# An SSD mixer's decay masks: one add and ten biased exps per block instead of ten subtractions and one exp, a fused state recurrence, and both directions' inputs formed in a row

## The chip, the cores and the metric

The kernel runs as one program on one core of a Trainium2 chip. Times are device microseconds (us) of one execution; the metric is their median. TensorE (PE) does the matrix products, VectorE (DVE), ScalarE (ACT) and GpSimd (POOL) the rest, SyncE (SP) issues most transfers. Each engine takes its instructions strictly in the order in which the program gives them to it.

## The reference

One step of a two-layer hybrid model on 640 tokens (128 context tokens, 512 latent ones), in 32-bit floats. Layer 0 runs a bidirectional Mamba-2 SSD mixer and an attention mixer, layer 1 an RG-LRU; each is followed by a gated FFN. The change lies in the SSD mixer alone. It has 16 heads of width 64 in 2 groups, states of 64, and works in 5 chunks of 128 tokens:

```
acs = jnp.cumsum(dtc * a, axis=2)
seg = acs[:, :, :, None] - acs[:, :, None, :]
lmat = jnp.exp(jnp.where(tril, seg, -jnp.inf))
xdt = xc * dtc[..., None]
cb = jnp.einsum('bcqgn,bckgn->bcqkg', cc, bc)
y_diag = jnp.einsum('bcqkg,bcqkgh,bckghp->bcqghp', cb, lmat, xdt)
decay_end = jnp.exp(acs[:, :, -1:] - acs)
states = jnp.einsum('bckgn,bckgh,bckghp->bcghpn', bc, decay_end, xdt)
h = chunk_decay * h + states          # chunk after chunk, from h0
y_off = jnp.einsum('bcqgn,bcghpn,bcqgh->bcqghp', cc, prev, jnp.exp(acs))
```

The backward direction does the same on the flipped sequence, and the two y are added.

## The kernel before

Every 32-bit product is made of three matmuls on split operands (`mm3`, lines 470 to 472, 128x322 each). The input projection of the SSD mixer makes 8 blocks of x and 8 of the gate z, each of 128 features, in the order of a hand-written plan; one call of `mm3` is one tick of a clock that exists only while the program is written. Beside it run three generators, each of which gives up its turn with `yield n` for n ticks (the table `SSD` holds the n). So the order of work on each engine is fixed by ticks and by conditions such as "y_done", not by time: whatever a generator issues at a tick stands in the engines' queues there, whether its data are ready or not.

- `mask_terms` forms for each block t of two heads (i counts the blocks) and each direction d the decay mask E (128 x 1280: 2 heads, 5 chunks of 128x128). The cumulative sums come broadcast by a DMA on SP (E<-ad, 640 KB), DVE takes the column's value off each 128x128 piece and clips at 88 (L1016, 10 instructions per direction), ACT takes one exp of the whole (L1017), and DVE multiplies by CBm (L1022), the product of C and B with the triangle already in it (made at L982, one per chunk and group). POOL then adds the two directions into M (L69). For each even block, Cs (exp on ACT at L1036, product with C on POOL, L69) serves two blocks; its two buffers are free for the next pair when the y of the block before have read them.
- `states` forms for each pair of blocks and each direction xw (DVE, L1057) in a single buffer, 8 products into the PSUM bank "o" (L1064), turns the final states on PE (L1071, L1072), copies them out on ACT (`fin` L1068, `ends` L1075), and runs the recurrence over chunks on DVE: a product (L1079) and an add from PSUM (L1082) per chunk, 128x128 each.
- `y_terms` multiplies M and Cs with x and the states (PE L1107, L1113) into a wide PSUM tile, and DVE folds the result into X (L317), then times zt (L1123).

Around them on the same queues: for each x block, ACT starts the convolution (L520) and DVE adds three taps (L317), later ACT takes silu (L1152), PE transposes (L1138), ACT copies to xtk (L1140); for each z block ACT evacuates with silu (zt, L1160), which frees one of two PSUM banks `gh`; ACT splits each weight block (whi, L112), POOL makes the rest (wlo, L117). Pieces of the modulation vector are also made here: four column-blocks of products on PE (L332) into a small PSUM bank `mt`, added on DVE (L340), and at an end transposed (L347) and added to a bias (L352). `mt` tiles sit in two banks, "m" and "o"; one is free for the next user when the last reader is done.

Of the kernel before, what the change touches and what calls it, by code (L numbers as in the profile page):

```python
# [9 lines left out]
F32 = mybir.dt.float32  # L10
F32R = mybir.dt.float32r
AF = mybir.ActivationFunctionType
# [9 lines left out]
NT = S0 + NS  # L22
# [218 lines left out]
def tile_hybrid_step(ctx: ExitStack, tc: tile.TileContext, a, o):  # L241
# [618 lines left out]

    def softplus(pool, out, x, sign, n):

        t = pool.tile([128, 4, n], F32, name="sp", tag="xw", bufs=1)
        ax, e, z, p = [t[:, i] for i in range(4)]
        nc.scalar.activation(ax, x, AF.Abs)
        nc.scalar.activation(e, ax, AF.Exp, scale=-1.0)
        nc.vector.tensor_scalar(ax, e, 2.0, None, op0=OP.add)
        nc.vector.reciprocal(z, ax)
        nc.vector.tensor_mul(z, z, e)
        nc.vector.tensor_mul(ax, z, z)  # L870
        nc.vector.tensor_scalar(p, ax, 1.0 / 15, None, op0=OP.mult)
        for c in (13, 11, 9, 7, 5, 3):
            fma(p, p, 1.0 / c, ax, op0=OP.add, op1=OP.mult)
        fma(p, p, 1.0, z, op0=OP.add, op1=OP.mult)
        nc.vector.tensor_scalar(e, x, float(sign), 0.0, op0=OP.mult, op1=OP.max)
        fma(out, p, 2.0, e, op0=OP.mult, op1=OP.add)
# [26 lines left out]
    def ssd(ctx2, ps):  # L903
# [6 lines left out]
        CT = conv(pool, ps[1], "ssd_cw", "ssd_cb", 4, 9, 10, "CT", 1)  # L910
        nc.scalar.activation(BT, BT, AF.Silu)
        nc.scalar.activation(CT, CT, AF.Silu)
        dtT = pool.tile([32, NT], F32, name="dtT", tag="xw")

        def dt_out(p, c0, c1):
            nc.scalar.copy(dtT[:, c0:c1], p[:32])
# [4 lines left out]
        wst = pool.tile([128, 160], F32, name="wst")  # L921
        cd = pool.tile([128, 5, 2, 8], F32, name="cd")
        Btok = pool.tile([128, 5, 128], F32, name="Btok")
        CBm = pool.tile([128, 5, 2, 2, 128], F32, name="CBm")
        acsT = pool.tile([32, 640], F32, name="acsT", tag="xw")
        ad = dpool.tile([32, 640], F32, name="ad")
        xtk, zt, Ms, Cs = {}, {}, {}, {}
        k.y_done = 0
# [1 line left out]
        def col(v, c, d, t, h):  # L930
            i = 32 * c + 16 * d + 2 * t + h
            return v[:, i:i + 1]

        def prep():
            m = mtile()
            for c, (c0, c1) in enumerate(CHUNKS):
                nc.tensor.transpose(m[:, 32 * c:32 * c + 32], dtT[:, c0:c1], ident[:32, :32])
            x = k.ldt = pool.tile([128, 160], F32, name="dA")
            nc.vector.tensor_add(x.rearrange("p (c h) -> p c h", c=5), m[:, :160].rearrange("p (c h) -> p c h", c=5),
                                 dtb[:, None, :].to_broadcast([128, 5, 32]))  # L940
            softplus(pool, dt, x, 1, 160)
            nc.vector.tensor_mul(x.rearrange("p (c h) -> p c h", c=5), dt.rearrange("p (c h) -> p c h", c=5),
                                 nega[:, None, :].to_broadcast([128, 5, 32]))
            yield SSD[0]
            m, m2 = mtile(), mtile()
            for c in range(5):
                for d in range(2):
                    q = slice(32 * c + 16 * d, 32 * c + 16 * d + 16)
                    nc.tensor.matmul(m[:, q], tri[:, d], x[:, q], start=True, stop=True)
            nc.tensor.matmul(m2[:, :160], ones, x, start=True, stop=True)  # L950
            nc.scalar.copy(acs, m[:, :160])
            nc.vector.tensor_sub(wst, m2[:, :160], acs)
            mv = m2[:, :160].rearrange("p (c d g h) -> p c d g h", c=5, d=2, g=2)
            for g in range(2):
                nc.scalar.activation(cd[64 * g:64 * g + 64], mv[64 * g:64 * g + 64, :, :, g], AF.Exp)
            nc.scalar.activation(wst, wst, AF.Exp)
            nc.vector.tensor_mul(wst, wst, dt)
            nc.vector.tensor_scalar(x, dt, 1e-38, None, op0=OP.max)
            nc.scalar.activation(x, x, AF.Ln)
            nc.vector.tensor_sub(x, acs, x)  # L960
            yield SSD[1]
            m, m2 = mtile(), mtile()
            for c in range(5):
                t = m[:32, 128 * c:128 * c + 128] if c < 4 else m2[:32, :128]
                nc.tensor.transpose(t, acs[:, 32 * c:32 * c + 32], ident)
            nc.vector.tensor_copy(acsT[:, :512], m[:32])
            nc.vector.tensor_copy(acsT[:, 512:], m2[:32, :128])
            nc.scalar.dma_start(ad, acsT)
            yield SSD[2]
            m, m2 = mtile(), mtile()  # L970
            for c, (c0, c1) in enumerate(CHUNKS):
                t = m[:, 128 * c:128 * c + 128] if c < 4 else m2[:, :128]
                nc.tensor.transpose(t, BT[:, c0:c1], ident)
            nc.vector.tensor_copy(Btok[:, :4], m.rearrange("p (c n) -> p c n", c=4))
            nc.vector.tensor_copy(Btok[:, 4], m2[:, :128])
            yield SSD[3]
            for c, (c0, c1) in enumerate(CHUNKS):
                for g in range(2):
                    m = mtile()
                    r = slice(64 * g, 64 * g + 64)  # L980
                    nc.tensor.matmul(m[:, :128], BT[r, c0:c1], CT[r, c0:c1], start=True, stop=True)
                    nc.vector.tensor_mul(CBm[:, c, :, g], tri, m[:, None, :128].to_broadcast([128, 2, 128]))  # L982
                yield SSD[4]

        def heads(t, d, n, part, c0, nt):
# [4 lines left out]
        def mask_terms():  # L990
# [14 lines left out]
            for i, t in enumerate(order):  # L1005
                until2 = i - 1
                while k.y_done < until2:
                    yield 1
                es = pend.pop(t)
                if i + 1 < 8:  # L1010
                    load(order[i + 1])
                for d in range(2):
                    for h in range(2):
                        for c in range(5):
                            v = es[d][:, h, 128 * c:128 * c + 128]
                            nc.vector.tensor_scalar(v, v, col(k.ldt, c, d, t, h), 88.0, op0=OP.subtract, op1=OP.min)  # L1016
                    nc.scalar.activation(es[d], es[d], AF.Exp)  # L1017
                    yield SSD[5]
                for d in range(2):
                    for h in range(2):  # L1020
                        v = es[d][:, h].rearrange("p (c q) -> p c q", c=5)
                        nc.vector.tensor_mul(v, v, CBm[:, :, d, t // 4])  # L1022
                    yield SSD[6]
                if i % 2 == 0:
                    while k.y_done < i:
                        yield 1
                    cs = []
                    for d in range(2):
                        q = pool.tile([128, 2, 512], F32, name="Cs", tag="Cs", bufs=2)
                        for g in range(2):  # L1030
                            heads(t + 4 * g, d, 64, q[64 * g:64 * g + 64], 128, 512)
                        cs.append(q)
                    Cs[t] = Cs[t + 4] = cs
                    yield SSD[7]
                    for q in cs:
                        nc.scalar.activation(q, q, AF.Exp)  # L1036
                        for h in range(2):
                            pieces(nc.gpsimd, "tensor_mul", q[:, h], q[:, h], CT[:, S0:])
                mm = Ms[t] = pool.tile([128, 2, 640], F32, name="M", tag="M", bufs=2)
                for h in range(2):  # L1040
                    pieces(nc.gpsimd, "tensor_add", mm[:, h], es[0][:, h], es[1][:, h])
                yield SSD[8]
# [3 lines left out]
        def states():  # L1046

            for i in range(4):
                ts = (i, 4 + i)
                while not k.prepared or any(t not in xtk for t in ts) or k.y_done < 2 * i - 2:  # L1050
                    yield 1
                S = [[None] * 5, [None] * 5]
                for d in range(2):
                    xw = pool.tile([128, 2, 5, 2, 64], F32, name="xw", tag="xw", bufs=1)
                    for j, t in enumerate(ts):
                        w = wst.rearrange("p (c e h) -> p c e h", c=5, e=2)[:, :, d, 2 * t:2 * t + 2, None]
                        nc.vector.tensor_mul(xw[:, j], xtk[t].rearrange("p c (h e) -> p c h e", h=2),  # L1057
                                             w.to_broadcast([128, 5, 2, 64]))
                    yield SSD[9]
                    m = mtile("o")  # L1060
                    cs = (0, 1, 2, 3) if d == 0 else (0, 4, 3, 2)
                    for n, c in enumerate(cs):
# [13 lines left out]
                    for n in range(1, 4):  # L1076
                        c, c2 = cs[n], (cs[n] + 1 if d == 0 else cs[n] - 1)
                        s = S[d][c2] = pool.tile([128, 128], F32, name="S", tag="S", bufs=16)
                        nc.vector.tensor_mul(s.rearrange("p (h e) -> p h e", h=2),  # L1079
                                             S[d][c].rearrange("p (h e) -> p h e", h=2),  # L1080
                                             cd[:, c, d, 2 * i:2 * i + 2, None].to_broadcast([128, 2, 64]))
                        nc.vector.tensor_add(s, s, m[:, 128 * n:128 * n + 128])  # L1082
                    yield SSD[11]
                Ss[i] = S

# [875 lines left out]
```

## Time and profile before

| | |
|---|---|
| time, median of 3 runs | 2131.27 us (2123.99 to 2131.78) |
| profiled execution | 2128.0 us, span 2126.2 us |
| PE busy | 1891.4 us, 89% of the span |
| DVE busy | 1467.3 us, 69% |
| POOL busy | 1208.1 us, 57% |
| ACT busy | 964.2 us, 45% |

The span is what the trace covers; the time has 1.8 us more around it. An engine's busy share is a mean over all stages; the lines that the diff touches run between about 115 and 320 us of the span. In the rows below, a line such as `E<-E,dA` names the tile written and the tiles read, `x10` the instructions grouped, and the bracket the idle time of the engine before the group with what ended it.

### The profile page before, as it was taken

How to read it: one execution, taken by the hardware profiler on the slowest of the kernel's cores; microseconds unless marked ns; L12 is line 12 of the kernel's file. 1: busy time of each engine (PE TensorE's matmuls, PEld its weight loads, DVE VectorE, ACT ScalarE, POOL GpSimd, SP SyncE). 2: the span in 40 equal slices, each digit the busy share in tenths (PEclk: the TensorE clock that was granted, in tenths of full speed). 3: DMA queues.
4: the chain of work that ended last, by engine and by line, in shares of the span. 5: the costliest groups of instructions: out<-in, count | busy, mean ns of one | idle time of the engine just before them, and what ended most of it. 6: DMA issues, size and time to landing. Idle time of an engine off the chain costs nothing.

```text
span 2126.2 us, 33767 instructions
## 1 busy us (share of the span) xinstructions
PE 1891.4 (89%) x12665; PEld 1735.7 (82%) x12665; DVE 1467.3 (69%) x2486; ACT 964.2 (45%) x1671; POOL 1208.1 (57%) x1542
## 2 busy tenths in 40 slices
PE   6878889999999988999999997977778799999997
PEld 4767768888888878799889997977678799999986
DVE  3477755656664357687777876788857778777874
ACT  3454444454553334343333444766724444343445
POOL 3335454333343535466666775688755577766772
PEclk9889999999999999999999998989789899999998
DMA  9545432121113431444542222111111122222221
GB/s 267 165 156 164 149 110 63 49 54 48 49 45 124 131 117 64 136 130 153 178 145 70 60 84 79 53 39 45 40 50 41 37 79 82 86 76 70 60 85 65
DMA packets 255578, 196.60 MB, mean 92 GB/s; under 512 B 13837, under 2 KB 233816, under 8 KB 255288
## 3 DMA queue, kind: packets, MB, share of 16 engines
q1 hardware_dynamic: 252664, 184.59, 28.9%
q0 software_dynamic: 2528, 7.13, 1.4%
q8 instruction: 100, 1.64, 0.3%
q10 hardware_dynamic: 224, 2.73, 0.3%
q14 instruction: 62, 0.51, 0.1%
HBM read 187.50 MB, written 6.92 MB: 91 GB/s over the span
## 4 chain that ended last, share of the span: by engine, by line
PE 36%; DVE 11%; POOL 9%; ACT 4%; issue 4%; DMA 4%; POOLq 0%; DVEq 0%; ACTq 0%; SPq 0%
PE wide L470 10%; PE wide L471 10%; PE wide L472 10%; POOL t L69 4%; POOL wlo L117 4%; DMA wraw<-in_ffn_w_up_dram 4%; DVE ft L317 2%; PE mt L332 1%; PE gh L470 1%; DVE X L317 1%; PE gh L471 1%; PE gh L472 1%; DVE wsum L141 1%; DVE wraw L140 1%; DVE wsum L139 1%
## 5 line engine op out<-in xcount | busy, mean ns | idle before, releaser
L117 POOL TENSOR_TENSOR wlo<-wraw,whi 128x256 fp32r<-128x256 f32 (+1 forms) x845 | 715.7, 875 | 544.7 <-ACT whi L112 476.8
L470 PE MATMUL wide<-hhi,whi 128*128 128x322 f32 (+4 forms) x1072 | 352.5, 329 | 49.5 <-DVE X L317 23.0
L471 PE MATMUL wide<-hlo,whi 128*128 128x322 f32 (+4 forms) x1072 | 345.8, 323 | 3.7 <-DVE hlo L511 3.4
L472 PE MATMUL wide<-hhi,wlo 128*128 128x322 f32 (+4 forms) x1072 | 343.1, 320 | 0.0
L112 ACT CAST whi<-wraw 128x1024 fp32r<-128x1024 f32 (+2 forms) x263 | 220.1, 839 | 150.4 <-PE wide L472 71.9
L470 PEld LDWEIGHTS wide<-hhi,whi 128*128 128x128 f32 x1072 | 213.2, 199 | 66.4 <-issue 21.6
L470 PE MATMUL gh<-hhi,whi 128*128 128x322 f32 (+3 forms) x704 | 236.7, 336 | 9.1 <-ACT zt L1160 8.6
L471 PE MATMUL gh<-hlo,whi 128*128 128x322 f32 (+3 forms) x704 | 221.2, 314 | 1.3 <-DVE hlo L511 1.0
L472 PE MATMUL gh<-hhi,wlo 128*128 128x322 f32 (+3 forms) x704 | 220.5, 313 | 0.0
L471 PEld LDWEIGHTS wide<-hlo,whi 128*128 128x128 f32 x1072 | 212.6, 198 | 6.1 <-DVE hlo L511 5.3
L472 PEld LDWEIGHTS wide<-hhi,wlo 128*128 128x128 f32 x1072 | 212.4, 198 | 0.0
L470 PE MATMUL wide<-hidh,whi 128*128 128x322 f32 (+4 forms) x624 | 199.7, 320 | 2.2 <-DVE ft L1584 2.2
L471 PE MATMUL wide<-hidl,whi 128*128 128x322 f32 (+4 forms) x624 | 195.5, 313 | 1.6 <-DVE hidl L511 1.6
L472 PE MATMUL wide<-hidh,wlo 128*128 128x322 f32 (+4 forms) x624 | 195.4, 313 | 0.0
L317 DVE SCALAR_TENSOR_TENSOR ft<-ft,PC 128x643 f32<-128x643 f32 x160 | 168.2, 1072 | 37.3 <-ACT ft L1526 35.3
L470 PEld LDWEIGHTS gh<-hhi,whi 128*128 128x128 f32 (+1 forms) x704 | 134.0, 190 | 34.7 <-issue 21.3
L1526 ACT ACTIVATE ft<-ft,PC 128x644 f32<-128x644 f32 x80 | 74.0, 927 | 144.4 <-DVE ft L1591 133.4
L317 DVE SCALAR_TENSOR_TENSOR X<-wide,modc,X 128x128 f32<-128x128 f32 (+3 forms) x264 | 123.5, 511 | 19.8 <-PE wide L472 19.8
L471 PEld LDWEIGHTS gh<-hlo,whi 128*128 128x128 f32 (+1 forms) x704 | 133.8, 190 | 2.4 <-DVE hlo L511 1.2
L472 PEld LDWEIGHTS gh<-hhi,wlo 128*128 128x128 f32 (+1 forms) x704 | 133.6, 190 | 0.6
L470 PEld LDWEIGHTS wide<-hidh,whi 128*128 128x128 f32 x624 | 118.7, 190 | 15.9 <-issue 7.0
L112 ACT CAST shi<-wsum 128x512 fp32r<-128x512 f32 x120 | 72.8, 617 | 124.3 <-DVE wsum L141 111.4
(386 smaller groups left out, 4676.4 us busy)
## 6 DMA issues: line engine op xcount, KB each, us to landing
wraw<-in_ffn_w_up_dram SPq DMA_DIRECT2D x88, 512.0 KB
mraw<-in_w_mod_dram SPq DMA_DIRECT2D x80, 512.0 KB
wraw<-in_ssd_attn_w_in_dram SPq DMA_DIRECT2D x42, 512.0 KB
wraw<-in_ffn_w_down_dram SPq DMA_DIRECT2D x96, 192.0 KB
E<-ad SPq DMA_DIRECT2D x16, 640.0 KB
mraw<-in_w_mod_dram SPq DMA_DIRECT2D x32, 256.0 KB
wraw<-in_ssd_attn_w_out_dram SPq DMA_DIRECT2D x16, 512.0 KB
wraw<-in_lru_w_in_dram SPq DMA_DIRECT2D x16, 512.0 KB
```

The source lines that it names most:

```text
L69: getattr(eng, op)(out[:, c], a[:, c], b[:, c])
L112: self.nc.scalar.copy(hi, src)
L117: low.tensor_sub(lo[:, q], src[:, q], hi[:, q].bitcast(F32))
L139: v.tensor_sub(s[:, 1], a[:, :4], b[:, :4])
L140: v.tensor_add(b[:, :4], b[:, :4], b[:, 4:])
L141: v.tensor_sub(s[:, 0], b[:, :4], a[:, :4])
L317: nc.vector.scalar_tensor_tensor(out, in0, scalar, in1, op0=op0, op1=op1, **kw)
L332: nc.tensor.matmul(m[32 * j:32 * j + 32, :256], scp[:, kt, :], raw[:, j * 256:(j + 1) * 256], start=half is None or kt == 0, stop=half is ...
L470: nc.tensor.matmul(ps[:whi.shape[-1], p0:p0 + c1 - c0], whi, xhi[:, c0:c1], start=start, stop=False)
L471: nc.tensor.matmul(ps[:whi.shape[-1], p0:p0 + c1 - c0], whi, xlo[:, c0:c1], start=False, stop=False)
L472: nc.tensor.matmul(ps[:whi.shape[-1], p0:p0 + c1 - c0], wlo, xhi[:, c0:c1], start=False, stop=stop)
L1526: after(at, lambda: nc.scalar.activation(out, u, AF.Identity, scale=par(cw, 2 * NF + t), bias=par(cb, t)))
```

## The change

Four things change. CB now holds the product of C and B without the triangle (ACT copies it from PSUM), and a tile `none` (0 inside the triangle, -1e30 outside, per direction) is added to E by DVE, one instruction per direction. The subtraction becomes the bias of the exp, so ACT runs ten exps of 128x128 per direction in place of one of 128x1280. The recurrence is one instruction per chunk and head (product and add in one, reading PSUM, 128x64). And xw has two buffers, both directions are formed one after the other, and the products of direction 1 follow 2 ticks behind the chain of direction 0. Lines after the edits move by up to 8.

```diff
@@ softplus, allocations
-        t = pool.tile([128, 4, n], F32, name="sp", tag="xw", bufs=1)
+        t = pool.tile([128, 4, n], F32, name="sp", tag="xw", bufs=2 if n > 16 else 1)
-        CBm = pool.tile([128, 5, 2, 2, 128], F32, name="CBm")
+        CB = pool.tile([128, 5, 2, 128], F32, name="CB")
+        none = pool.tile([128, 2, 128], F32, name="none")
@@ prep
+            nc.vector.tensor_scalar(none, tri, 1.0, 1e30, op0=OP.subtract, op1=OP.mult)
-            nc.vector.tensor_sub(x, acs, x)
+            nc.vector.tensor_sub(x, x, acs)
-                    nc.vector.tensor_mul(CBm[:, c, :, g], tri, m[:, None, :128].to_broadcast([128, 2, 128]))
+                    nc.scalar.copy(CB[:, c, g], m[:, :128])
@@ mask_terms
                 for d in range(2):
+                    v = es[d].rearrange("p h (c q) -> p (h c) q", c=5)
+                    nc.vector.tensor_add(v, v, none[:, d, None, :].to_broadcast([128, 10, 128]))
+                for d in range(2):
                     for h in range(2):
                         for c in range(5):
                             v = es[d][:, h, 128 * c:128 * c + 128]
-                            nc.vector.tensor_scalar(v, v, col(k.ldt, c, d, t, h), 88.0, op0=OP.subtract, op1=OP.min)
-                    nc.scalar.activation(es[d], es[d], AF.Exp)
+                            nc.scalar.activation(v, v, AF.Exp, bias=col(k.ldt, c, d, t, h))
                     yield SSD[5]
                 for d in range(2):
                     for h in range(2):
                         v = es[d][:, h].rearrange("p (c q) -> p c q", c=5)
-                        nc.vector.tensor_mul(v, v, CBm[:, :, d, t // 4])
+                        nc.vector.tensor_mul(v, v, CB[:, :, t // 4])
                     yield SSD[6]
@@ states
+                xws = []
                 for d in range(2):
-                    xw = pool.tile([128, 2, 5, 2, 64], F32, name="xw", tag="xw", bufs=1)
+                    xw = pool.tile([128, 2, 5, 2, 64], F32, name="xw", tag="xw", bufs=2)
...
-                    yield SSD[9]
+                    xws.append(xw)
+                    yield SSD[9] if d else 2
+                for d, xw in enumerate(xws):
                     m = mtile("o")
...
                     for n in range(1, 4):
                         c, c2 = cs[n], (cs[n] + 1 if d == 0 else cs[n] - 1)
                         s = S[d][c2] = pool.tile([128, 128], F32, name="S", tag="S", bufs=16)
-                        nc.vector.tensor_mul(s.rearrange("p (h e) -> p h e", h=2),
-                                             S[d][c].rearrange("p (h e) -> p h e", h=2),
-                                             cd[:, c, d, 2 * i:2 * i + 2, None].to_broadcast([128, 2, 64]))
-                        nc.vector.tensor_add(s, s, m[:, 128 * n:128 * n + 128])
+                        for h in range(2):
+                            e = slice(64 * h, 64 * h + 64)
+                            fma(s[:, e], S[d][c][:, e], cd[:, c, d, 2 * i + h:2 * i + h + 1],
+                                m[:, 128 * n + 64 * h:128 * n + 64 * h + 64])
                     yield SSD[11]
```

**First place.** ACT's queue where the first masks are made (the silu of an x block lies between the two directions), before:

```order
L735 ACTIVATE lv<-lv 128x2
L1017 ACTIVATE E<-E 128x1280
L1152 ACT_TABLE_LOAD
L1152 ACTIVATE X<-X 128x644
L1017 ACT_TABLE_LOAD
L1017 ACTIVATE E<-E 128x1280
L1068 COPY fin<-mt 128x128
L1140 COPY xtk<-wide 128x640
```

and after the change:

```order
L735 ACTIVATE lv<-lv 128x2
L1021 ACTIVATE E<-E,dA 128x128 x10
L1159 ACT_TABLE_LOAD
L1159 ACTIVATE X<-X 128x644
L1021 ACT_TABLE_LOAD
L1021 ACTIVATE E<-E,dA 128x128 x10
L1147 COPY xtk<-wide 128x640
L1075 COPY fin<-mt 128x128
```

The silu keeps its place behind the first direction's exps, which are now ten; on PE the state products (L1064, now L1071) have moved from two ticks ahead of the transposes of that X (L1138, now L1145) to behind them.

**Second place.** PE at the third y pass (tile M_1739, the first block of the second pair). Before, the transposes of an X block come first and the pass begins 5 ticks later:

```order
L1071 MATMUL mt_1801<-ident_68,ends1_463 128x128
L1072 MATMUL mt_1801<-ident_68,fin_1742 128x128
L470 MATMUL wide_1703<-hhi7_81,whi_1383 128x322
L471 MATMUL wide_1703<-hlo7_89,whi_1383 128x322
L472 MATMUL wide_1703<-hhi7_81,wlo_1384 128x322
L470 MATMUL wide_1703<-hhi7_81,whi_1383 128x322
L471 MATMUL wide_1703<-hlo7_89,whi_1383 128x322
L472 MATMUL wide_1703<-hhi7_81,wlo_1384 128x322
L1138 MATMUL wide_1822<-ident_68,X_73 128x128 x5
L332 MATMUL mt_1830<-mraw_1491,scp_118 32x256 x4
```

and after the change the pass stands in the middle of the x block's own products (wide_1716):

```order
L472 MATMUL wide_1716<-hhi6_80,wlo_1397 128x322
L1114 MATMUL wide_1808<-M_1739,xtk_1217 64x128 x4
L1120 MATMUL wide_1808<-Cs_1677,S_1619 64x128 x2
L1120 MATMUL wide_1808<-Cs_1680,S_1765 64x128 x2
L470 MATMUL wide_1716<-hhi7_81,whi_1396 128x322
L471 MATMUL wide_1716<-hlo7_89,whi_1396 128x322
L472 MATMUL wide_1716<-hhi7_81,wlo_1397 128x322
```

The states are ready earlier in the program, and the pass begins 18 ticks of projection behind the end of the second pass, where there were 25. The transposes (wide_1871 now) follow it.

**Third place.** ACT's queue where the fifth block's masks meet the states of the third pair (fin and ends are the copies of final states), before:

```order
L1036 ACTIVATE Cs_2093<-Cs_2093 128x1024
L1075 COPY ends0_460<-mt_2151 128x128
L1017 ACTIVATE E_1952<-E_1952 128x1280
L1017 ACTIVATE E_1954<-E_1954 128x1280
L1068 COPY fin_2240<-mt_2231 128x128
L112 CAST whi_2250<-wraw_1845 128x1024
```

and after:

```order
L1040 ACTIVATE Cs_2098<-Cs_2098 128x1024
L1082 COPY ends0_460<-mt_2162 128x128
L1075 COPY fin_2192<-mt_2183 128x128
L1021 ACTIVATE E_1980<-E_1980,dA_800 128x128 x10
L1021 ACTIVATE E_1982<-E_1982,dA_800 128x128 x10
L1082 COPY ends1_463<-mt_2244 128x128
L112 CAST whi_2267<-wraw_1860 128x1024
```

The second `ends` copy, which frees the bank mt_2244 for PE's next L332, now stands right behind the twenty exps; before, `fin` stood there and `ends` came later.

## Rows read from the trace of the kernel before

**Rows 1.** SSD stretch: busy us of PE, PEld, DVE, ACT, POOL; granted clock, DMA share, GB/s.
```profile
119.00:320.00 201.00, 166.53 (x1325) 137.91 (x1324) 143.64 (x330) 92.88 (x111) 98.39 (x137) 0.92 0.48 147
```

**Rows 2.** PE's waits from 119 to 320 us: total us, times, longest.
```profile
PE mt L332 <- issue: 10.6, 2, 7.4
PE gh L470 <- ACT zt L1160: 8.6, 4, 6.2
PE mt L1064 <- DVE xw L1057: 6.2, 1, 6.2
PE mt L1071 <- DVE macc L340: 4.4, 1, 4.4
PE mt L332 <- ACT ends L1075: 2.8, 2, 2.2
PE wide L1138 <- ACT X L1152: 1.2, 1, 1.2
```

**Rows 3.** Groups by line and shape, 85 to 330 us: busy us, mean ns | idle before.
```profile
L1016 DVE TENSOR_SCALAR E<-E,dA 128x128 f32<-128x128 f32 x160 | 54.1, 413 | 5.4 <-DMA E<-ad 5.4
...
L1017 ACT ACTIVATE E<-E 128x1280 f32<-128x1280 f32 x16 | 20.1, 1270 | 27.6 <-DVE E L1016 19.6 <-POOL M L69 7.8
...
L1079 DVE TENSOR_TENSOR S<-S,cd 128x128 f32<-128x128 f32 x24 | 9.3, 389 | 0.8
...
L1082 DVE TENSOR_TENSOR S<-S,mt 128x128 f32<-128x128 f32 x24 | 6.9, 288 | 1.0
```

**Rows 4.** DVE in order of time at the first masks (start, us of the group).
```profile
126.22 2.05 DVE L1016 TENSOR_SCALAR E<-E,dA 128x128 f32<-128x128 f32 x10 [5.36 <-DMA E<-ad]
128.18 1.55 DVE L1057 TENSOR_TENSOR xw<-xtk,wst 128x640 f32<-128x640 f32 x2
```

**Rows 5.** DVE in order of time, fifth block.
```profile
230.90 2.10 DVE L1057 TENSOR_TENSOR xw<-xtk,wst 128x640 f32<-128x640 f32 x2
232.92 9.86 DVE L1016 TENSOR_SCALAR E<-E,dA 128x128 f32<-128x128 f32 x20
```

**Rows 6.** POOL in order of time in the same stretch.
```profile
230.96 6.79 POOL L69 TENSOR_TENSOR Cs<-Cs,CT 128x256 f32<-128x256 f32 x8 [1.10 <-issue]
```

**Rows 7.** ACT in order of time, layer 1: 128x128 instructions with a bias from a tile.
```profile
1302.42 0.69 ACT L600 ACTIVATE hhi<-sqt,modc 128x128 fp32r<-128x128 f32 x2 [0.40 <-DVE sqt L317]
```

**Rows 8.** ACT in order of time at the first masks.
```profile
129.59 1.28 ACT L1152 ACT_TABLE_LOAD   x1
130.88 0.74 ACT L1152 ACTIVATE X<-X 128x644 f32<-128x644 f32 x1
```

**Rows 9.** PE in order of time at the first masks.
```profile
122.46 0.31 PE L471 MATMUL wide<-hlo,whi 128*128 128x322 f32 x1
122.61 0.30 PE L472 MATMUL wide<-hhi,wlo 128*128 128x322 f32 x1
...
132.12 0.47 PE L471 MATMUL wide<-hlo,whi 128*128 128x322 f32 x1
132.39 0.47 PE L472 MATMUL wide<-hhi,wlo 128*128 128x322 f32 x1
```

**Rows 10.** PE in order of time: end of the second y pass.
```profile
175.97 0.65 PE L1113 MATMUL wide<-Cs,S 64*64 64x128 f32 x8
```

**Rows 11.** SP's issues in the same stretch.
```profile
176.45 2.54 SPq L988 DMA_DIRECT2D Cs<-ad  x4
```

**Rows 12.** ACT in order of time behind them.
```profile
183.69 1.06 ACT L1036 ACTIVATE Cs<-Cs 128x1024 f32<-128x1024 f32 x1 [1.28 <-DMA Cs<-ad]
```

**Rows 13.** POOL in order of time behind that.
```profile
183.03 5.61 POOL L69 TENSOR_TENSOR Cs<-Cs,CT 128x256 f32<-128x256 f32 x8
188.60 3.67 POOL L69 TENSOR_TENSOR M<-E 128x213 f32<-128x213 f32 x6
```

**Rows 14.** DVE in order of time, seventh block, and what follows it.
```profile
288.33 10.30 DVE L1016 TENSOR_SCALAR E<-E,dA 128x128 f32<-128x128 f32 x20
298.55 0.23 DVE L352 TENSOR_TENSOR modc<-mt,PC 128x8 f32<-128x8 f32 x2
```

More of the change, by code (lines that the diff above doesn't have):

```diff
@@ L912, in ssd @@
         nc.scalar.activation(CT, CT, AF.Silu)
-        dtT = pool.tile([32, NT], F32, name="dtT", tag="xw")
+        dtT = pool.tile([32, NT], F32, name="dtT", tag="xw", bufs=2)
         def dt_out(p, c0, c1):
@@ L923, in ssd @@
         Btok = pool.tile([128, 5, 128], F32, name="Btok")
-        CBm = pool.tile([128, 5, 2, 2, 128], F32, name="CBm")
-        acsT = pool.tile([32, 640], F32, name="acsT", tag="xw")
+        CB = pool.tile([128, 5, 2, 128], F32, name="CB")
+        none = pool.tile([128, 2, 128], F32, name="none")
+        acsT = pool.tile([32, 640], F32, name="acsT", tag="xw", bufs=2)
         ad = dpool.tile([32, 640], F32, name="ad")
```

## The prediction

> **What bounds it now.** I read the page first: PE is busy 89% of the span, so time comes only from stretches in which PE waits or works slowly. The diff touches one such stretch, 119 to 320 us. There PE is busy 166.5 of 201 us at a mean granted clock of 0.92, DVE 143.6, ACT 92.9, POOL 98.4 [rows 1]. So 34.5 us without work on PE is the most that waits can give back; the six groups of PE's waits hold 33.8 of it [rows 2]. Who ends them matters more than their sum. The 6.2 us on xw (L1057), the 4.4 on macc (L340) and the 10.6 put down to "issue" (two waits of L332) all stand behind DVE: the longest of the last kind ends with the small adds of L352, which DVE could only run when twenty subtractions in a row were done [rows 14]. The other waits, 8.6 on zt, 2.8 on ends, 1.2 on X, end with ACT; but ACT's exps in turn waited 19.6 us for the subtractions [rows 3]. DVE is thus what PE waits for, directly or at one remove, and the change takes work from it. The question is what stands there next.
>
> **What a wait costs beside itself.** After a long wait PE's matmuls follow each other every 0.27 us (132.12 to 132.39) instead of every 0.15 [rows 9], the lower of the two clock levels, 1.2 in place of 2.4 GHz, for some 3.5 us: about 1.6 us lost for each long wait. I count five such waits before and five or six after, so this adds 0 to 3.
>
> **DVE's share.** Gone: 160 subtractions, 54.1 us; 24 products and 24 adds of the recurrence, 9.3 and 6.9 [rows 3]; ten CBm products, which I leave out of the sum. Added: 16 adds of 128x1280. Two 128x640 instructions with two SBUF inputs take 1.55 us [rows 4], so one add is about 1.5 with POOL idle. With POOL at work on Cs, two take 2.10 [rows 5, 6]: about 2.05 per add. Added too: 48 fused steps of 128x64, no row like them; below the 0.29 of L1082, which also reads PSUM (128x128), above half of it, so 7 to 14 us, and I take 10 (a fixed part per instruction does not halve). DVE is relieved by 70.3 - 16 x 1.75 - 10 = 32 us. None of it is on PE's path by itself.
>
> **ACT's share.** 16 exps of 1270 ns [rows 3] become 160 of 128x128 with the bias from a tile. The nearest row is L600, the same shape and operand: two take 0.69 us [rows 7]. If the first takes 0.39 and the next follows at 0.30, ten take 3.1; if both count 0.345, 3.45. I take 3.1 per direction, 6.1 for the twenty of a block against 2.5 before: ACT gains 160 x 0.30 - 20.3 = 28 us. The Trainium skill, "ScalarE: Activation LUTs", section "What ACT_TABLE_LOAD costs", speaks against this split: a biased ACTIVATE costs about 280 ns + 0.833 per element, 93 ns of it overlapped back to back, an estimate of 0.294 each and 3.0 for ten, while one over all 1280 columns would pay the fixed part once; the sum would be smaller by 0.2 us per block of waits than mine. Ten CB copies are added, at about 0.26 each.
>
> So the way from a landed E to its finished exps becomes: with POOL idle, before 20 x 0.2 + 1.3 = 5.4 us [rows 4], after 1.5 + 6.1 = 7.6. With POOL busy, before 9.9 to 10.3 + 1.3 = 11.4 [rows 5, 14], after 2.05 + 6.1 = 8.2. **The load moves from DVE's queue into ACT's**, and ACT's queue carries the silus, zt, xtk and the copies that free PSUM banks. I went through PE's program tick by tick and asked at each step what it waits for.
>
> 1. *First masks.* DVE's first subtraction waited for E's DMA until 126.22 [rows 4]; PE waited 6.24 at L1064. Now DVE adds until 127.7, the ten exps of direction 0 end near 130.9, table load 1.28 and silu 0.74 follow [rows 8], and only then can PE transpose X: about 133.2. PE runs the two ticks that it had behind L1064 first and stands from 123.9: 9.3 us in place of 6.2. **+3.1.**
> 2. *The bank "o".* Direction 1's products come two ticks (0.9 us) behind direction 0's transposes and need the bank that the recurrence still reads: a copy of 0.29 and six steps of about 0.25, so 0.9 us of waiting at least where DVE is free, up to 2.9 where three convolution taps are ahead. Four pairs: 2.6, 0.3, 1.0, 1.0 by what is ahead of each. **+4.9** (0 to 8).
> 3. *zt and the first L332 behind DVE.* The 6.2 us on zt shrinks to about 1.9, since direction 1's exps no longer wait for DVE; the 3.2 us on L332 to 0.6, since the subtractions ahead of it are gone. **-6.9.**
> 4. *Third y pass.* PE meets it 18 ticks of 0.44 after the end of the second pass (176.6, [rows 10]), with a small product and transposes near 185.5. But the second pass frees the Cs buffers, SP issues the loads then [rows 11], the second lands 183.69 for its exp [rows 12], POOL multiplies until 188.6 and makes M until 192.3 [rows 13]. Before, 25 ticks and two waits covered this. PE waits about 7, and the transposes behind it another 2.3 for the convolution that was held up by the pass in its middle; the 2.2 on ends [rows 2] and 0.4 of the small zt waits go. **+6.9.**
> 5. *Third pair of states.* Before, 4.4 on macc and about 2.4 of small waits. Now PE's L332 needs the bank that the ends copy frees, behind twenty exps: 6.3. **-0.5.**
> 6. *Seventh silu.* Twenty exps now stand ahead of a silu that had run before them: 6.1 and a table load, less what PE has to do meanwhile, 6.2; before 1.2 + 0.7. **+4.3.**
> 7. *Last L347.* Before, 7.4 behind the 10.30 of subtractions [rows 14]. Now it waits for the ends copy behind twenty exps: 7.1. **-0.3.**
>
> Sum: 3.1 + 4.9 - 6.9 + 6.9 - 0.5 + 4.3 - 0.3 = +11.5, less 0.5 for DVE's small jobs done earlier: **+11 us**. On the profiled execution's 2128.0 that is 2139; that execution lies 3 us under the median of 2131.27 and inside the three runs, so against the median the same sum would say 2142. I stay with 2139.
>
> **Rivals.**
> - *A, DVE's relief wins.* The 27 us that end with DVE (6.2, 4.4, 10.6 and 6.2 of zt) go and what replaces them is short, because every chain now starts earlier: E is free and added to earlier, so the exps are done before PE comes to the ends copies, and M before the third pass. For it: with POOL busy a block's masks are ready 3 us sooner, and ACT was busy only 92.9 of 201 [rows 1]. Against it: the exps stand in the queue just ahead of what PE needs, whatever ACT's mean. It decides at steps 5 to 7: if their waits are at most 2 us each, 15 us go, and without step 4's 7 as well, the time is 2139 - 15 - 7 = 2117; if in step 2 nothing waits either, 2112.
> - *B, even.* The new waits are as long as the old: steps 2 and 6 at their lower ends (0 and 1) take 10 off the sum: 2129.
> - *C, the sum:* 2139, own range 2130 to 2147.
> - *D, POOL is the new bound.* If the contended add costs like the subtractions with POOL (4.9 per direction rather than 2.05) and POOL's M is late in the same measure, steps 4 to 6 grow by about 4 each, and two more half-clock stretches cost 3: 2154.
>
> **Chances.** About 0.5% (10.6 us) is what a measurement of this kernel can tell from no change. A 0.20, B 0.24, C 0.44, D 0.12. C straddles the bound: half of it counts as slower. Faster 0.20 (A), same 0.24 + 0.22 = 0.46, slower 0.22 + 0.12 = 0.34. The range 2116 to 2152 leaves out the far half of A and of D.
>
> **What would show it.** Right: ten L1021 in about 3.1 us; waits of PE on the silu near 124 to 133 of 9 us, on POOL's M in the third pass of about 7, and on the ends copy of 6 to 7 twice; no wait on xw or macc. DVE's busy time in the stretch down by some 30 us, ACT's up by as much. Wrong: if PE's waits in the stretch sum to under 25 us, A holds, and the queue-order argument for steps 5 to 7 was misjudged; if L1021's pitch is 0.22 or lower, steps 1, 5, 6, 7 shrink by 1 to 2 us each; if adds under POOL take 4 us or more, D.

## The result

The changed kernel takes 2141.4 us (median of 8 runs, 2135.73 to 2147.35) against 2128.86 for the kernel before in the same session: a ratio of 1.006, 95% interval 1.0043 to 1.0077. The forecast was 2139, range 2116 to 2152. It is slower by 0.6%; the time is the one forecast, but made up of other parts.

The profiled execution took 2139.54 us, 11.5 more than the one of before. From 332 us on it runs as before did from 320 on, to within 1 us; so the loss lies in the stage of the masks and in what directly follows it. That stage, in the view of busy time and granted clock (PE, PEld, DVE, ACT, POOL, then clock, DMA share, GB/s), against [rows 1]:

```profile
119.00:332.00 213.00, 176.71 (x1342) 143.59 (x1341) 118.66 (x180) 116.36 (x254) 117.01 (x139) 0.88 0.46 142
```

DVE did 25 us less, ACT 23 more, as the change intends; POOL's 19 more are longer instructions, not more work: wlo (52 each time) took 49.5 us for 38.5, the products with C (32) 30.6 for 25.5. PE was without work for 213 - 176.7 = 36.3 us, before for 34.5: only 1.8 more. But its clock was 0.88 in place of 0.92: 213 x 0.12 = 25.6 us lost, before 201 x 0.08 = 16.1. So 9.5 of the 11.3 us are in the clock column. (Two decimals of the clock leave about 1 us open on each side. Counted from the first transposes of acs to the last product of the last y pass, the stage takes 225.8 us against 216.2; PE's idle time there grew by 1.6, the lost clock by 8.5.) This is not one execution's accident: the mean granted clock over the whole run is 0.9447 over the eight runs and 0.950 over 70 runs of the kernel before, and 0.005 of 2140 us is 11 us. PE's waits, total us, times, longest, against [rows 2]:

```profile
PE wide L1145 <- ACT X L1159: 12.9, 2, 7.3
PE wide L1114 <- POOL M L69: 6.3, 2, 5.2
PE mt L347 <- ACT ends L1082: 5.5, 1, 5.5
PE mt L332 <- ACT ends L1082: 3.8, 1, 3.8
PE mt L1071 <- DVE S L317: 2.9, 3, 1.3
PE wide L1145 <- DVE X L317: 2.2, 1, 2.2
PE gh L470 <- ACT zt L1167: 2.0, 1, 2.0
```

None of the waits on xw, macc or the "issue" of L332 is left, and in their place stand silus, ends copies and M, about as long in all. The durations, from the groups by line (busy us, mean ns), against [rows 3]:

```profile
L1021 ACT ACTIVATE E<-E,dA 128x128 f32<-128x128 f32 x160 | 48.0, 389 | 8.9 <-DVE E L1016 8.9
L1026 DVE TENSOR_TENSOR E<-E,CB 128x640 f32<-128x640 f32 x32 | 30.7, 998 | 4.4 <-ACT E L1021 4.4
L1016 DVE TENSOR_TENSOR E<-E,none 128x1280 f32<-128x1280 f32 x16 | 26.3, 1680 | 4.4 <-DMA E<-ad 4.3
L317 DVE SCALAR_TENSOR_TENSOR S<-S,cd,mt 128x64 f32<-128x64 f32 x48 | 9.9, 275 | 0.5
```

One exp counts 0.30 us in a row of them (48.0 / 160), one add 1.64, one fused step 0.21, all as costed. The multiplications by CB became slower (998 against a mean of 818 ns before): 22 of the 32 still take 0.81 to 0.83 us, the other ten 1.26 to 1.96, and all ten ran while POOL was at work for half of their time or more.

The dearest place is the third y pass. At the 169th L470 of the trace the changed kernel is 6.4 us ahead of before (182.6 against 189.0 us); at the 203rd, when both have run the pass, it is 3.9 behind (224.0 against 220.1). PE there, in order of time:

```profile
190.56 0.69 PE L1114 MATMUL wide<-M,xtk 128*64 128x128 f32 x2 [5.16 <-POOL M L69]
192.34 1.28 PE L1114 MATMUL wide<-M,xtk 128*64 128x128 f32 x6 [1.09 <-POOL M L69]
...
204.21 1.30 PE L1145 MATMUL wide<-ident,X 128*128 128x128 f32 x5 [2.17 <-DVE X L317]
```

and the same stretch by 5 us (columns as above; the clock is the third figure from the end):

```profile
185.00:190.00 5.00, 0.40 (x3) 0.14 (x1) 2.29 (x2) 4.96 (x14) 5.00 (x6) 1.00 0.05 16
190.00:195.00 5.00, 3.34 (x17) 1.98 (x18) 0.00 (x0) 3.30 (x12) 3.47 (x6) 0.52 0.10 29
195.00:200.00 5.00, 5.00 (x34) 3.35 (x37) 0.00 (x0) 1.83 (x2) 2.48 (x4) 0.50 0.60 233
200.00:205.00 5.00, 2.83 (x15) 1.64 (x13) 3.92 (x6) 0.00 (x0) 0.30 (x1) 0.50 0.61 178
205.00:210.00 5.00, 5.00 (x26) 4.01 (x25) 3.30 (x6) 2.72 (x3) 0.89 (x1) 0.50 0.13 35
```

PE stood for almost all of 185 to 190 and then worked at 1.2 GHz for some 20 us, two more waits of 1.1 and 2.2 us included; it was back at 2.4 after 210. POOL, for which it stood, was itself held up beside the new adds on DVE (183.4 to 187.3): eight products took 8.04 us where they took 5.61 before [rows 13]. The two that ran beside the adds took 1.97 us each, the other six 0.72 to 0.74.

```profile
181.88 8.04 POOL L69 TENSOR_TENSOR Cs<-Cs,CT 128x256 f32<-128x256 f32 x8 [0.46 <-POOL wlo L117]
189.88 3.59 POOL L69 TENSOR_TENSOR M<-E 128x213 f32<-128x213 f32 x6
```

### The profile page after: what moved, and what is told of

Same layout as the page of the kernel before. It is cut to its first block, busy times and chain, and to the rows that moved or that the text cites. A ratio compares the mean times of both kernels' runs of the same rounds, so it can differ in the third digit from the quotient of the medians.

```text
span 2137.8 us, 33774 instructions
## 1 busy us (share of the span) xinstructions
PE 1900.3 (89%) x12665; PEld 1741.5 (81%) x12665; DVE 1437.8 (67%) x2333; ACT 988.4 (46%) x1821; POOL 1224.5 (57%) x1542
## 3 DMA queue, kind: packets, MB, share of 16 engines
q8 instruction: 100, 1.64, 0.3%
## 4 chain that ended last, share of the span: by engine, by line
PE 33%; DVE 12%; POOL 10%; ACT 5%; DMA 4%; issue 4%; POOLq 0%; DVEq 0%; SPq 0%; ACTq 0%
PE wide L470 9%; PE wide L471 9%; PE wide L472 9%; POOL wlo L117 4%; DMA wraw<-in_ffn_w_up_dram 4%; POOL t L69 4%; DVE ft L317 2%; PE gh L470 1%; PE mt L332 1%; PE gh L471 1%; DVE X L317 1%; PE gh L472 1%; DVE wraw L140 1%; DVE wsum L141 1%; DVE wsum L139 1%
## 5 line engine op out<-in xcount | busy, mean ns | idle before, releaser
L117 POOL TENSOR_TENSOR wlo<-wraw,whi 128x256 fp32r<-128x256 f32 (+1 forms) x845 | 725.3, 887 | 536.3 <-ACT whi L112 465.1
L470 PE MATMUL wide<-hhi,whi 128*128 128x322 f32 (+4 forms) x1072 | 352.7, 329 | 51.4 <-DVE X L317 24.6
L470 PEld LDWEIGHTS wide<-hhi,whi 128*128 128x128 f32 x1072 | 212.9, 199 | 69.3 <-issue 24.1
L470 PE MATMUL gh<-hhi,whi 128*128 128x322 f32 (+3 forms) x704 | 239.1, 340 | 2.6 <-ACT zt L1167 2.0
L470 PE MATMUL wide<-hidh,whi 128*128 128x322 f32 (+4 forms) x624 | 200.1, 321 | 2.2 <-DVE ft L1591 2.2
L317 DVE SCALAR_TENSOR_TENSOR ft<-ft,PC 128x643 f32<-128x643 f32 x160 | 168.2, 1072 | 37.4 <-ACT ft L1533 35.4
L470 PEld LDWEIGHTS gh<-hhi,whi 128*128 128x128 f32 (+1 forms) x704 | 135.8, 193 | 29.5 <-issue 22.8
L317 DVE SCALAR_TENSOR_TENSOR X<-wide,modc,X 128x128 f32<-128x128 f32 (+3 forms) x264 | 123.5, 511 | 19.7 <-PE wide L472 19.7
L470 PEld LDWEIGHTS wide<-hidh,whi 128*128 128x128 f32 x624 | 119.2, 191 | 15.9 <-issue 6.6
```

The lines of the kernel that those rows point to most:

```text
L117: low.tensor_sub(lo[:, q], src[:, q], hi[:, q].bitcast(F32))
L317: nc.vector.scalar_tensor_tensor(out, in0, scalar, in1, op0=op0, op1=op1, **kw)
L470: nc.tensor.matmul(ps[:whi.shape[-1], p0:p0 + c1 - c0], whi, xhi[:, c0:c1], start=start, stop=False)
```

## The experiments

Each median is of 5 to 12 runs, beside runs of the kernel before on the same chip (medians 2128.0 to 2129.3). "Clock" is the mean granted clock over all runs of a kernel. One interval spans 2 to 5 us to either side, so differences of 3 to 5 us between two changed kernels are not resolved.

| kernel | median us | ratio to before (95%) | clock |
|---|---|---|---|
| before | 2128 to 2129 | | 0.950 |
| the change | 2141.4 | 1.0060 (1.0043 to 1.0077) | 0.9447 |
| masks alone | 2141.7 | 1.0066 (1.0050 to 1.0082) | 0.9447 |
| fused recurrence alone | 2126.5 | 0.9990 (0.9980 to 1.0000) | 0.9490 |
| change, one exp, DVE forms the sum | 2145.3 | 1.0084 (1.0066 to 1.0102) | 0.9452 |
| change, third pass 16 ticks later | 2135.8 | 1.0041 (1.0022 to 1.0060) | 0.9465 |
| change, PE's waits filled | 2142.8 | 1.0065 (1.0053 to 1.0077) | 0.9490 |
| change, silu 3 ticks earlier | 2149.9 | 1.0094 (1.0080 to 1.0109) | 0.9438 |
| change, ends on DVE | 2141.6 | 1.0069 (1.0045 to 1.0092) | 0.9442 |
| change, third pass 16 later, ends on DVE | 2127.6 | 1.0002 (0.9981 to 1.0022) | 0.9487 |
| change, third pass 28 later, ends on DVE | 2132.7 | 1.0016 (1.0003 to 1.0029) | 0.9466 |
| change, 16 later, ends on DVE, silu earlier | 2130.6 | 1.0013 (0.9996 to 1.0029) | 0.9476 |
| masks alone, one wait filled (two runs) | 2141.9, 2137.7 | 1.0063 (1.0046 to 1.0080), 1.0051 (1.0031 to 1.0071) | 0.9463, 0.9493 |

My first theory after the result was that the third y pass, put nearer to the second, is the loss, with its clock; the rival that it is the exps in ACT's queue.

**1. The masks alone** (the kernel before, with only the CB, `none` and bias edits, together).

> The kernel before with the masks and exps of the change alone (add of none, ten biased exps per direction, CB copied by ACT); recurrence, xw and the program's order of states and y passes stay as before. Theory (the loss comes from the third y pass, put 7 ticks nearer to the second, and the low clock that follows its waits): 2131 us, 2126 to 2136, with no wait of PE on POOL's M over 1.5 us at the third pass. Rival (the loss comes from the exps in ACT's queue, ahead of silus and ends copies): the whole loss is here, 2138 to 2144 us.

The whole loss is here, 2141.7 us: the rival's number, and my theory in that form fell, since here the third pass stands where it stood before. But the profile is not the rival's either. PE's stage and its waits:

```profile
119.00:332.00 213.00, 180.74 (x1327) 147.28 (x1326) 123.06 (x184) 120.76 (x256) 114.09 (x137) 0.86 0.44 136
```
```profile
PE gh L470 <- ACT zt L1164: 11.1, 4, 6.3
PE mt L1068 <- DVE xw L1061: 6.4, 1, 6.4
PE mt L332 <- ACT ends L1079: 4.4, 2, 3.6
PE mt L332 <- issue: 4.4, 2, 2.5
PE wide L1142 <- ACT X L1156: 3.4, 2, 2.7
PE mt L1076 <- ACT fin L1072: 2.5, 1, 2.5
```

PE waits less than before (213 - 180.7 = 32.3 us against 34.5): the two long waits behind DVE's twenty subtractions went from 10.6 to 4.4 in all. All of the stage's loss in this execution is clock: 213 x 0.14 = 29.8 us against 16.1. (Another 6 us of this execution lie behind the stage, in code that both kernels share.) The longest low stretches are where before had none: after waits of 2.5, 2.7 and 0.8 us between 246 and 257, PE ran at 1.2 GHz from 258 to 275, and after one of 1.5 us from 285 to 299. The six executions agree: their clock is 0.942 to 0.947, and 0.005 less of 2140 us is 11 of the 13 us.

**2. The fused recurrence alone** (the kernel before, with the six lines of `fma` in place of product and add).

> The kernel before with the fused recurrence alone. 24 products and 24 adds (16.2 us of DVE) become 48 steps of 0.2 to 0.28 us (9.9 to 13). Both theories: within 0.3% of the kernel before, 2123 to 2134 us; the waits of PE behind DVE change by under 1 us each.

2126.5 us, ratio 0.999 with an interval that ends at 1.000: a gain of 0 to 4 us, as expected. It is the one part that is not a loss. PE's waits behind DVE changed by more than the expected 1 us (xw 6.2 to 4.2, macc 4.4 to 3.1), while those on ends grew from 2.8 to 4.7.

xw with two buffers was not measured alone. As masks alone and the whole change measure the same, the order of the states adds nothing that can be measured to the total, though it changes where the time is lost.

**3. One exp again, DVE forms the sum.**

```diff
-                    nc.vector.tensor_add(v, v, none[:, d, None, :].to_broadcast([128, 10, 128]))
-                            nc.scalar.activation(v, v, AF.Exp, bias=col(k.ldt, c, d, t, h))
+                            nc.vector.scalar_tensor_tensor(v, v, col(k.ldt, c, d, t, h), none[:, d], op0=OP.add, op1=OP.add)
+                    nc.scalar.activation(es[d], es[d], AF.Exp)
```

> The changed kernel with ten DVE instructions per direction that add the column's value and the mask in one step (128x128), and one exp of 128x1280 on ACT as before; all else as changed. Theory: the third pass still stands where it did, so most of the loss stays; waits on silu and ends shrink by some 8 us and those behind DVE return by as much: 2135 to 2145 us. Rival (ACT's exps are the loss): back to the time of the kernel before, 2125 to 2131.

2145.3 us, no better than the change: with the rest of the change in place, taking the ten exps out of ACT's queue gives nothing back. DVE's step of 128x128 took 464 ns on average (62.4 us for 160), more than the subtraction's 413 [rows 3]; PE waited 12.2 on two silus, 7.7 and 2.6 on ends, 3.9 on M and 3.9 on macc. So the waits on silus and ends did not shrink by the 8 us that I expected. The number of exps on ACT is not by itself the loss: the ten exps without the new order (masks alone) and the new order without the ten exps (this run) each cost all of it. That the same things are now late because of DVE is argued, not shown.

**4. The third pass later.**

```diff
-                    yield SSD[12]
+                    yield SSD[12] + (16 if i == 1 and g == 0 else 0)
```

> The changed kernel with the third y pass held back by 16 more ticks of the program's clock. Theory: PE's waits on POOL's M (6.3 us in two) and on the convolution behind it (2.2) go, and the low-clock stretch of 20 us after 190 shrinks to 7 or less; 2141 - 8 - 5 = 2128 us, 2124 to 2134. Rival (ACT's exps): the pass only waits elsewhere, under 4 us gained, 2137 to 2142.

2135.8 us: 5.6 gained, between the two expectations. By the ratios it is 4, and the two intervals overlap. The waits on M and on the convolution went; PE was 19 us ahead of the change at one point, but with the pass still to do, and then ran into a silu's wait of 3.1 us and 14 us of low clock (201 to 215). In this profile 7 us were left at the end of the stage.

**5. PE's waits filled** with products whose results are overwritten.

```diff
             g = wide()
+            for _ in range({1: 44, 2: 12, 7: 34}.get(t, 0)):
+                nc.tensor.matmul(g[:, :322], H[0][0][:, :128], H[0][0][:, :322], start=True, stop=True)
...
                     y = wide()
+                    for _ in range({1: 32}.get(t, 0)):
+                        nc.tensor.matmul(y[:, :322], H[0][0][:, :128], H[0][0][:, :322], start=True, stop=True)
```

> The changed kernel with idle matmuls (128x322, about 0.15 us each, results overwritten) put on PE where it waits: 44, 12 and 34 ahead of the transposes of the third, fifth and last X blocks, 32 ahead of the third y pass; outputs as before. The places where PE waits, and for whom, stay. Theory (the clock): the waits end at the same instants, but the low-clock stretches behind them (10, 20 and 7 us) shrink by half or more; 2141 - 10 = 2131 us, 2126 to 2136. Rival (the length of the waits alone counts): 2139 to 2145, since the idle matmuls fill time that was lost anyway.

The time is the rival's, 2142.8 us; the clock over the runs is 0.949, nearly that of before. In its profile no low stretch stands behind the first and the last silu any more, but the one at the third pass is still 17 us long (20 in the change):

```profile
119.00:332.00 213.00, 185.94 (x1435) 154.18 (x1434) 113.96 (x176) 115.25 (x250) 113.42 (x138) 0.91 0.45 135
198.00:203.00 5.00, 4.80 (x31) 2.59 (x31) 1.22 (x2) 0.94 (x2) 2.77 (x4) 0.50 0.22 61
```

After the first silu PE, faster there, came sooner to the next thing that was not ready: the wait on the bank "o" grew from 1.3 to 3.8. The one on ends grew from 3.8 to 5.7, though PE came to it 3 us later than in the change.

```profile
PE mt L332 <- ACT ends L1082: 5.7, 1, 5.7
PE mt L347 <- ACT ends L1082: 5.5, 1, 5.5
PE mt L1071 <- DVE S L317: 5.4, 3, 3.8
```

The run does not decide between theory and rival, though, since the idle products cost time of their own. They took 20.3 us, while PE's waits fell by only 9.2 (36.3 to 213 - 185.9 = 27.1). The twelve ahead of the fifth block's transposes filled no wait at all:

```profile
204.97 3.56 PE L1147 MATMUL wide<-hhi 128*128 128x322 f32 x12 [2.17 <-DVE X L317]
```

Here the wait for the convolution comes ahead of them as well, since they write the same PSUM bank as the transposes, and at 1.2 GHz they then took 3.6 us. Over the whole stage 20.3 us of products, less 9.2 of waits and some 7 of regained clock, come to the 4.2 us by which this stage is longer than the change's (230.0 against 225.8). So the regained clock may well have been worth its time. That a regained clock is lost again at the next wait is seen at the bank "o" (2.5 us of the wait), not for the whole stage.

**6. Silu earlier.**

```diff
-SSD = (25, 6, 9, 1, 2, 3, 3, 5, 9, 10, 9, 2, 6, 1, 6, 10)
+SSD = (25, 6, 9, 1, 2, 3, 3, 5, 9, 10, 9, 2, 6, 1, 3, 13)
```

> The changed kernel with ACT's silu of each x block issued 3 ticks earlier (3 instead of 6 behind the projection, the transposes where they were), so that it stands ahead of the exps of the first and of half those of the seventh block. Theory (the order in ACT's queue makes PE wait, and each such wait brings a low-clock stretch): waits on silu from 12.9 to 3 us or less, and 5 of clock: 2141 - 14 = 2127 us, 2122 to 2133. Rival (the time is only moved on to the next wait): 2137 or more.

2149.9 us, the slowest of all. The wait on the first silu did go (12.9 us of silu waits became 2.7), but ACT now stands for DVE's convolution, and what is queued behind it is late: zt costs PE 10.3 us, xw 4.7, M 8.5. The time is the rival's. A step moved ahead of a full queue blocks the queue itself when its own input is not ready: the next silu kept ACT idle for 2.8 us.

**7. Ends on DVE, alone, with the later pass, and more.**

```diff
-                    nc.scalar.copy(ends[d][:, i], m2[:, 128:256].rearrange("p (g n) -> p g n", g=2))
+                    nc.vector.tensor_copy(ends[d][:, i], m2[:, 128:256].rearrange("p (g n) -> p g n", g=2))
```

> The changed kernel with the ends copies on DVE in place of ACT. Theory (a bank that frees only behind twenty exps makes PE wait, 3.8 and 5.5 us, and a low-clock stretch of 3 and 7 us stands behind each): 2141 - 9 - 4 = 2128 us, 2125 to 2134, as the end of the stage has no other wait near. Rival (the time moves on to the next wait): 2137 or more.

> The changed kernel with the third y pass 16 ticks later and the ends copies on DVE, silu where the change has it. Theory (both losses are separate and add): 2141.4 - 5.6 - 10 = 2126 us, 2120 to 2130. Rival (one is given back in the other): 2132 or more.

> As the kernel with the third pass 16 ticks later and the ends copies on DVE, but 28 ticks later. Theory (the pass loses by its closeness to POOL's M and the silu and convolution beside it): 2120 to 2128 us, no low-clock stretch over 7 us near 200. Rival (the pass itself brings the low clock, wherever it stands): the stretch of 13 us comes along with the pass, and the time stays within 2 us of the 16 ticks.

> The changed kernel with three edits: silu 3 ticks earlier, the third y pass 16 ticks later, and the ends copies on DVE in place of ACT (so that the bank they free does not wait for twenty exps). Theory: silu waits 10 us less, M and convolution 8 less, ends 7 less, and some 12 of low clock less; 2105 to 2122 us, faster than the kernel before. Rival (the waits move on): 2125 to 2135.

Alone it gains nothing (2141.6): the two waits on ends are gone (5.5 and 3.8 became 0.7 and 0.6), but the fifth pass, reached sooner, waits 3.3 us for one of DVE's L317 steps, and the clock is as low as in the change: the rival's result. Together with the later pass it gains 13.8 us, against 5.6 and 0 for the two apart: 2127.6, as expected, and level with the kernel before. The stage of this kernel, and PE's waits:

```profile
117.00:317.00 200.00, 172.20 (x1314) 138.19 (x1314) 119.25 (x191) 113.66 (x243) 115.64 (x136) 0.89 0.46 143
```
```profile
PE wide L1145 <- ACT X L1159: 16.6, 3, 8.1
PE mt L1071 <- DVE S L317: 4.2, 3, 2.5
PE wide L1114 <- DVE X L317: 2.2, 1, 2.2
```

200 us, as before, with 27.8 us of waiting in place of 34.5 and 22 us of clock in place of 16. So the loss is mended by taking away two things that the change had put in PE's way, when both go; a gain over before does not appear. Why the pair gives back more than its parts is not shown. With twelve ticks more the median is 5 us higher, outside both expectations: no low stretch over 7 us is left near 200, but M is waited for again (9.1 us, at a later pass), with 24 us of low clock from 247 on. With the earlier silu on top it is 3 higher, the rival's time; both differences are within the intervals. No version here beats the kernel before.

**8. The masks alone with one wait filled**, 16 products ahead of the transposes of the seventh X block, and the same once more.

> The kernel before with the masks of the change alone, and 16 idle matmuls (128x322, 2.4 us) on PE in the 2.7 us in which it waits for the silu of the last X block but one; outputs as before. Theory (the low clock behind several short waits is the loss, not the waits): the low-clock stretch of 17 us from 258 shrinks by half or more, PE is 4 us ahead behind it, and 2136 to 2140 us remains, as the next long wait takes some of it back. Rival (the silu's lateness sets the end, whatever the clock): within 1 us of the masks alone, 2141 to 2144.

> The kernel with the masks alone and 16 idle matmuls once more, for a second profiled execution and more times. If the 16 matmuls keep the clock up in every execution: stage (from the transposes of acs to the last product of the last y pass) again 216 to 219 us with under 30 us at the low clock. Rival (where the clock falls differs from execution to execution, and one profile is one draw): stage 222 us or more, over 40 us at the low clock, and a median of 2139 to 2144 us again.

In both profiles the low stretch from 258 (251 in the second) is gone and the stage, from the transposes of acs to the last product of the last y pass, is short: 217.4 and 217.5 us, against 227.9 for the masks alone and 216.2 before. The first, of the stage and of 5 us pieces of it,

```profile
119.00:322.00 203.00, 169.44 (x1346) 140.18 (x1345) 122.86 (x186) 122.28 (x258) 115.16 (x139) 0.93 0.48 148
255.00:260.00 5.00, 5.00 (x48) 3.22 (x40) 4.28 (x9) 2.14 (x4) 5.00 (x9) 1.00 0.73 224
260.00:265.00 5.00, 5.00 (x45) 4.00 (x44) 2.21 (x3) 1.87 (x2) 0.56 (x1) 1.00 0.69 204
```

where the kernel without the products had

```profile
255.00:260.00 5.00, 3.80 (x23) 2.24 (x23) 4.53 (x11) 2.90 (x5) 4.19 (x6) 0.79 1.02 310
260.00:265.00 5.00, 5.00 (x30) 3.25 (x30) 1.94 (x3) 2.03 (x2) 2.81 (x5) 0.50 0.33 92
265.00:270.00 5.00, 5.00 (x30) 3.09 (x29) 0.00 (x0) 0.00 (x0) 0.00 (x0) 0.50 0.90 330
```

So in these two executions 2.6 us of idle products kept the clock up through the 17 us that follow, and the stage was 10 us shorter. The medians, 2141.9 and 2137.7, are only 0 and 4 us better than without the products, and the single runs say why. The profiled executions have the highest clock of their six each, 0.951 and 0.952. Of the twelve executions, four have a clock of 0.950 or more and take 2134 us in the mean; the other eight have 0.945 to 0.948 and take 2142, as the six without the products do (0.942 to 0.947, 2142). So the time does go with the clock, but in most executions the products did not raise it. Where it fell in those is not known, as they were not profiled. The first median is the rival's; in the second run the stage is as expected for products that keep the clock up, the time is not the rival's either.

## Why the prediction came out, and where its steps did not

- **The sum.** 2139 against 2141.4, and 0.6% where it said 0.5 (of its verdicts it held "same" likelier than "slower", 0.46 to 0.34). That the number came out is luck: it was made of waits (+11) and of 0 to 3 us of clock, and the profile divides it as 1.8 of waits and 9.5 of clock. Two errors of some 9 us cancel. The new waits were each costed too long or about right, 45.6 us in all, and measured about 36. The step that failed is "what a wait costs beside itself": I priced each long wait at 3.5 us of low clock and counted waits. In the trace of before the wait that I read it from has a low stretch of 6.8 us (128.2 to 135.0), and there are six stretches, 34 us in all or 17 of lost clock, where five times 1.6 makes 8. The changed kernel has 51 us of them, 20 at the third pass alone, and the masks alone got 17 and 14 us from waits of under 3 us, which I had not counted as long at all.
- **Step 1** (9.3): 7.3, since E's data were there 2.8 us sooner than assumed (1 us of that because this execution runs 1 us earlier up to there); the order add, ten exps, table load, silu was as costed, with the ten exps in 3.03 us where the working has 3.1. **Step 2** (4.9): 2.9, in three places. **Step 3** (1.9 and 0.6): 2.0 and 0.4. **Step 6** (6.2): 5.6.
- **Step 4** (9.3 in all): 6.3 on M and 2.2 on the convolution, 8.5. The right place, and with its clock the dearest; holding the pass back gives 4 to 6 us, more only when the ends copies go too.
- **Steps 5 and 7** (6.3 and 7.1): 3.8 and 5.5, right in kind, but together with the clock behind them worth nothing when taken away alone. The working added each wait as though PE's time behind it were free to keep; experiments 6 and 7 show waits removed and their time lost again, at the next things not ready or in the clock.
- **DVE's and ACT's shares**: -25 and +23 us in the stage against -32 and +28. On DVE it was missed that the products with CB (6 us) and those for xw (2.4) become slower; on ACT the exps cost the 28, but four table loads fewer took 5 off.
- **Rival A** (DVE's relief wins) was right that the waits that end with DVE go: 27 us became 5. It fell by its own tests: the waits of steps 5 to 7 are 3.8, 5.6 and 5.5 us, not at most 2, and PE's waits sum to 36.3, not to under 25. **Rival B** (the new waits are as long as the old) has the waits right, 36.3 for 34.5, and its 2129 misses the time by 12 us because it too had no price for the clock. **Rival D** asked for adds of 4.9 beside POOL; those took 1.95 to 2.03, as the sum had it (2.05). But that POOL would be late in turn, which D also said, is seen: 8.04 for 5.61 us.
- **What stays open**: why the masks alone, with less waiting on PE, bring down the clock. Their loss lies in the clock, in the profile (12 us of the stage) and in the mean of the six executions (11 us), and with one wait filled the executions in which the clock stays up are 7 us faster than those in which it does not. But it stayed up in four of twelve only, so what brings it down is not shown; nor were the three edits of the masks taken apart. In the changed kernel the two things that cost the time were found by taking both away; how much of that is waiting and how much clock is not settled.

## What to carry to other kernels

Work moved from one in-order queue to another moves the waits too: list what PE next needs from the queue that receives it (here silus, copies that free banks) before counting what the other is relieved of. A wait taken out alone can give nothing (here the ends copies), since PE arrives sooner at the next one; try the pair. And compare PE's idle time and its lost clock side by side before and after: either alone tells half. And compare the clock of every execution, not of the profiled one alone: here two profiles show a clock that most executions of the same kernel did not have.

## What the runs showed of the hardware that I had not expected

PE fell to 1.2 GHz after waits of 2.5, 2.7 and 0.8 us close together (masks alone, 258 us), and stayed there for 17 us, of which the pieces from 260 to 275 show it busy throughout; in two profiled executions with 16 idle products in one of these waits it stayed at 2.4. A biased 128x128 exp costs 0.30 us in a row, so ten cost 3.0 where one of 1280 columns costs 1.27. An add of 128x1280 from two SBUF tiles takes 1.49 us with POOL idle; two of them beside POOL's products took 1.95 and 2.01, and the two products beside them 1.97 us each where the others took 0.72 to 0.74.
